# State stage of a hybrid decoder trunk: one run of small steps and one of dense blocks in each gap of the chunk chain

## The chip, the cores and the metric

The kernel runs on one core of one Trainium2 chip. The metric is the device time of one execution in microseconds; times of a kernel are the median of several runs. The profile is one execution taken by the hardware profiler.

## The reference, cut to what matters

Two layers of a decoder trunk are computed for a prompt of 1024 positions and a sample group of 8 sequences with 4 positions each. Each layer has one combined projection, a recurrent branch (RWKV-7), an attention branch with a window of 128, a merge of both, and a feed-forward part with a short convolution. The part that matters here is the recurrence of the first branch, for 8 heads of size 64:

```python
def step(S, inp):
    r_t, w_t, k_t, v_t, kk_t, a_t = inp
    sk = jnp.einsum('bhvk,bhk->bhv', S, kk_t)
    S = (S * w_t[:, :, None, :]
         - sk[..., None] * (kk_t * a_t)[:, :, None, :]
         + v_t[..., None] * k_t[:, :, None, :])
    return S, jnp.einsum('bhvk,bhk->bhv', S, r_t)
```

All data is float32. The output has the trunk's result, the new states and the new caches.

## The kernel before, in words

The recurrence is computed in chunks of 64 positions. Inside a chunk it becomes matrix products with masked Gram matrices and the inverse of a triangular matrix; between chunks the state S is carried on. A layer has 16 chunks; two of them, 128 positions, are a group `sg` (0 to 7). In this document the chunks of a layer are numbered 0 to 15: group `sg` has the chunks 2`sg` and 2`sg`+1.

`m_chain` (line 682) is the chain of a group. For each chunk TensorE first multiplies values and old state into two PSUM tiles (lines 704 and 711), VectorE copies the sum to X (line 716), TensorE multiplies it with the inverse (line 720), ScalarE writes the result as U (line 723), TensorE forms the new state (line 726), which VectorE adds up (line 730), and the output (line 733), which ScalarE copies to Y (line 737). Between these steps TensorE would wait for the other engines. So `m_chain` calls `gap(i)` at three places of each chunk: 0 after X, 1 after U, 2 after Y. What `gap` puts there decides the order of TensorE's work, since the stage runs under a manual schedule for TensorE: its instructions stay in the order in which the program writes them. For the other engines the scheduler sets the order, by its own timeline.

Three generators and one block provide the work for the gaps:

- `fill()` issues one **dense block**: three matmuls of 128x128 by 352 columns (lines 383 to 385) of the combined projection, for parts that are used only after this stage. Eight blocks fill a PSUM tile, which VectorE scales to `gt` (line 390); their total number is fixed, and what is left over runs in the attention stage.
- `nxt` is `prep(sg + 1)`, the work ahead of the next group's chain. `m_front` (line 566) loads BK, RA and VV, forms four groups of Gram products (line 590), masks them on VectorE (line 600), scales BK on GpSimd (line 604), transposes BK (line 609) and VV (line 617), and ScalarE empties these tiles (lines 612, 614, 620). `m_comb` (line 655) combines the parts of the inverse in six steps (lines 668, 673, 678). A `yield` ends a step; `yield True` says that a block should follow before the next one.
- `smp` is `m_sample` (line 852), the same work for the sample group (lines 820 to 904). `post` is `m_post` (line 908), the normalisation of a finished group on VectorE and ScalarE and its transposes (line 933).
- `inv` is `m_invs` (line 627), the inverse for the group after next: 31 columns, each with a product and a subtraction on VectorE (lines 641 and 643), then two trips through DRAM. It yields after every `IV` = 7 columns.

`psG`, `psT`, `psV`, `psY`, `psS`, `psT1` are PSUM tiles of one pool with three banks; a fourth tile has to wait until the first of them has been emptied. The chain's own tiles `xb` and `sb` have a bank each, the dense blocks two.

`gap(i)` before (lines 770 to 776) issues `HK[i]` blocks, 6, 5 and 5, and behind each of the first three a small step, `side()`. That is 16 blocks and up to nine small steps a chunk. `side()` (lines 760 to 768) takes the steps from `nxt` first and later in a chunk pair mostly from `post` and `smp`. Behind the blocks of gaps 0 and 1 one call of `inv` emits seven columns.

Of the kernel before, what the change touches and what calls it, by code (L numbers as in the profile page):

```python
# [25 lines left out]
AD = (1, 4, 4)  # L26
SQ = ((1, 3, 5, 7),) * 3
MS = 20
HK = (6, 5, 5)
AK = (4, 2)  # L30
GPB = 2
OXB = 3
# [2 lines left out]
A0 = 24  # L35
PA = (2, 2, 3, 1)
M7 = 12
GN = (3, 3, 3)
GS = 3
IV = 7  # L40
PS = 5
L = 2
TP = 1024
NS = 8
# [89 lines left out]
class Trunk:  # L134
# [492 lines left out]
    def m_invs(self, l, sg):  # L627
# [9 lines left out]
        for j in range(31):  # L637
# [5 lines left out]
            V.tensor_tensor(R[:, 0:c, j + 1:32], R[:, 0:c, j + 1:32], tv, ALU.subtract)  # L643
            if j % IV == IV - 1:
                yield
# [98 lines left out]
    def m_stage(self, l, Ts):  # L744
        ms = [{} for _ in range(8)]

        def prep(sg):
            yield from self.m_front(l, sg, ms[sg])
            yield from self.m_comb(l, sg, ms[sg], Ts[sg])
        self.fill(MS)  # L750
        for _ in prep(0):
            self.fill(1)
        self.m_state()
        smp, post = self.m_sample(l), iter(())
        for sg in range(8):
            nxt = prep(sg + 1) if sg < 7 else iter(())
            n = [0]
            cur = [None]

            def side():  # L760
                n[0] += 1
                o = (nxt,) if not sg else (nxt, smp, post) if n[0] < PS else (smp, post, nxt) if n[0] % GS == 0 else (post, nxt, smp)
                for g in (cur[0],) if cur[0] else o:
                    r = next(g, 0)
                    if r == 0 and r is not False:
                        continue
                    cur[0] = g if r else None
                    return

            def gap(i):  # L770
                for k in range(HK[i]):
                    self.fill()
                    if k < GN[i]:
                        side()
                if i < 2:
                    next(inv, 0)
            inv = self.m_invs(l, sg + 2) if sg < 6 else iter(())
            next(nxt, 0)
            Y = self.m_chain(l, sg, ms[sg], gap)
            while cur[0]:  # L780
                self.fill()
                side()
            for _ in post:
                self.fill()
            for _ in nxt:
                self.fill()
            if sg < 6:
                Ts.append(list(inv)[-1])
            if sg == 0:
                for _ in range(5):  # L790
                    next(smp)
                    self.fill()
            post = self.m_post(l, sg, Y)
            next(post)
        for _ in smp:
            self.fill()
        self.fill(M7)
        for _ in post:
            self.fill()
# [846 lines left out]
```

## Time and profile before

| | |
|---|---|
| median of 3 runs | 3429.51 us (3418.05 to 3434.38) |
| profiled execution | 3434.58 us, span 3432.8 us |
| mean granted clock of TensorE | 0.972 of full speed |
| TensorE busy | 3270.1 us (95%) |
| VectorE busy | 2220.3 us (65%) |
| ScalarE busy | 1447.6 us (42%) |
| GpSimd busy | 1361.2 us (40%) |

The state stage runs twice, once in each layer. Counted from the start of the span, the chain of layer 0 starts at 324.7 us and its chunk 15 at 640.4 us; in layer 1 these are 2021.1 and 2333.0 us. The views below name engines PE (TensorE's matmuls), PEld (its weight loads), DVE (VectorE), ACT (ScalarE) and POOL (GpSimd). A clock of 1.00 is 2.4 GHz, one of 0.50 is 1.2 GHz; values between them are means over a stretch.

### The profile page before, as it was taken

How to read it: one execution, taken by the hardware profiler on the slowest of the kernel's cores; microseconds unless marked ns; L12 is line 12 of the kernel's file. 1: busy time of each engine (PE TensorE's matmuls, PEld its weight loads, DVE VectorE, ACT ScalarE, POOL GpSimd, SP SyncE). 2: the span in 40 equal slices, each digit the busy share in tenths (PEclk: the TensorE clock that was granted, in tenths of full speed). 3: DMA queues.
4: the chain of work that ended last, by engine and by line, in shares of the span. 5: the costliest groups of instructions: out<-in, count | busy, mean ns of one | idle time of the engine just before them, and what ended most of it. 6: DMA issues, size and time to landing. Idle time of an engine off the chain costs nothing. (4 is left out here: it accounts for less than half of the span.)

```text
span 3432.8 us, 67390 instructions
## 1 busy us (share of the span) xinstructions
PE 3270.1 (95%) x26254; PEld 3064.3 (89%) x26254; DVE 2220.3 (65%) x4183; ACT 1447.6 (42%) x2908; POOL 1361.2 (40%) x1440
## 2 busy tenths in 40 slices
PE   7999889999989999999999998899999899998998
PEld 7998668888989999999999986689889899998998
DVE  6677775375567777755547778735745677777554
ACT  4443223355444444445434432243643444444443
POOL 5541121132346666633245411111323466665332
PEclk9999889999999999999999998999999999999999
DMA  3335333444542222366623453335454422225664
GB/s 116 118 117 168 104 111 113 146 152 160 179 162 75 75 77 85 103 211 214 183 92 106 136 150 107 112 108 182 138 191 143 142 75 76 86 82 174 197 187 129
DMA packets 299711, 453.48 MB, mean 132 GB/s; under 512 B 86192, under 2 KB 215728, under 8 KB 299104
## 3 DMA queue, kind: packets, MB, share of 16 engines
q1 hardware_dynamic: 298240, 448.92, 41.2%
q8 instruction: 206, 3.38, 0.4%
q14 instruction: 113, 0.93, 0.1%
q10 hardware_dynamic: 1152, 0.26, 0.0%
HBM read 322.58 MB, written 128.53 MB: 131 GB/s over the span
## 5 line engine op out<-in xcount | busy, mean ns | idle before, releaser
L1262 PE MATMUL psA<-x,wh 128*128 128x264 f32 x1408 | 404.2, 287 | 31.0 <-ACT wh L1213 21.4
L231 PE MATMUL psd<-hi,wh 128*128 128x352 f32 x1248 | 407.4, 330 | 5.1 <-ACT hi L252 2.7
L233 PE MATMUL psd<-hi,wl 128*128 128x352 f32 x1248 | 407.2, 326 | 2.7 <-POOL wl L224 1.5
L232 PE MATMUL psd<-lo,wh 128*128 128x352 f32 x1248 | 406.9, 326 | 2.0 <-DVE lo L253 2.0
L1264 PE MATMUL psA<-x,wl 128*128 128x264 f32 x1408 | 403.2, 287 | 1.4 <-DVE wl L1214 1.4
L1263 PE MATMUL psA<-x,wh 128*128 128x264 f32 x1408 | 402.9, 286 | 0.0
L383 PE MATMUL psg<-hi,wh 128*128 128x352 f32 x1056 | 388.3, 368 | 7.9 <-DVE gt L390 7.9
L1213 ACT CAST wh<-wr 128x512 fp32r<-128x512 f32 (+1 forms) x420 | 246.3, 592 | 297.6 <-PE psd L1391 178.8
L384 PE MATMUL psg<-lo,wh 128*128 128x352 f32 x1056 | 350.5, 332 | 0.0
L385 PE MATMUL psg<-hi,wl 128*128 128x352 f32 x1056 | 348.9, 330 | 0.0
L1390 PE MATMUL psd<-ap,wh 128*128 128x352 f32 x1056 | 343.0, 325 | 5.5 <-ACT wh L1213 5.4
L1391 PE MATMUL psd<-ap,wh 128*128 128x352 f32 x1056 | 342.8, 325 | 1.8 <-DVE ap L1246 1.8
L1392 PE MATMUL psd<-ap,wl 128*128 128x352 f32 x1056 | 341.9, 324 | 0.1
L1214 POOL TENSOR_TENSOR wl<-wr,wh 128x512 fp32r<-128x512 f32 (+1 forms) x196 | 248.1, 1266 | 179.3 <-ACT wh L1213 174.8
L1262 PEld LDWEIGHTS psA<-x,wh 128*128 128x128 f32 x1408 | 268.1, 190 | 33.5 <-ACT wh L1213 22.0
L1214 DVE TENSOR_TENSOR wl<-wr,wh 128x512 fp32r<-128x512 f32 (+1 forms) x224 | 167.4, 752 | 189.4 <-ACT wh L1213 187.0
L1264 PEld LDWEIGHTS psA<-x,wl 128*128 128x128 f32 x1408 | 267.6, 190 | 2.2 <-DVE wl L1214 2.0
L1263 PEld LDWEIGHTS psA<-x,wh 128*128 128x128 f32 x1408 | 268.0, 190 | 0.2
L383 PEld LDWEIGHTS psg<-hi,wh 128*128 128x128 f32 x1056 | 203.3, 193 | 51.0 <-issue 28.9
L231 PEld LDWEIGHTS psd<-hi,wh 128*128 128x128 f32 x1248 | 235.9, 190 | 9.9 <-ACT wh L223 4.0
L233 PEld LDWEIGHTS psd<-hi,wl 128*128 128x128 f32 x1248 | 236.3, 189 | 5.0 <-DVE wl L224 2.3
L232 PEld LDWEIGHTS psd<-lo,wh 128*128 128x128 f32 x1248 | 236.7, 190 | 4.5 <-DVE lo L253 3.4
(356 smaller groups left out, 8567.1 us busy)
## 6 DMA issues: line engine op xcount, KB each, us to landing
wr<-wdn SPq DMA_DIRECT2D x96, 512.0 KB, 3.5
wr<-wff SPq DMA_DIRECT2D x88, 512.0 KB, 4.0
wr<-win SPq DMA_DIRECT2D x72, 512.0 KB, 3.7
ad<-ct SPq DMA_DIRECT2D x44, 528.0 KB, 2.9
ar<-ad SPq DMA_DIRECT2D x132, 176.0 KB, 3.3
td<-gt SPq DMA_DIRECT2D x96, 176.0 KB, 1.8
gl<-td SPq DMA_DIRECT2D x32, 528.0 KB, 4.6
wr<-wdn SPq DMA_DIRECT2D x40, 384.0 KB, 3.6
```

What stands on the lines that cost most here:

```text
L231: self.nc.tensor.matmul(ps, wh, xh[:, s], start=i == 0, stop=False)
L232: self.nc.tensor.matmul(ps, wh, xl[:, s], start=False, stop=False)
L233: self.nc.tensor.matmul(ps, wl, xh[:, s], start=False, stop=i == last)
L383: nc.tensor.matmul(ps, wh[:, k], hi[:, s], start=k == 0, stop=False)
L384: nc.tensor.matmul(ps, wh[:, k], lo[:, s], start=False, stop=False)
L385: nc.tensor.matmul(ps, wl[:, k], hi[:, s], start=False, stop=k == 7)
L1214: sub.tensor_tensor(lo, x, h.bitcast(F32), ALU.subtract)
L1262: nc.tensor.matmul(ps[c][:, 0:HC], w[0][:, ws], xh, start=first and i == 0, stop=False, skip_group_check=True)
L1263: nc.tensor.matmul(ps[c][:, 0:HC], w[0][:, ws], xl, start=False, stop=False, skip_group_check=True)
L1264: self.lastP = nc.tensor.matmul(ps[c][:, 0:HC], w[1][:, ws], xh, start=False, stop=end and i == 3, skip_group_check=True)
L1390: nc.tensor.matmul(ps, wh[:, ws], hi, start=k == 0, stop=False)
L1391: nc.tensor.matmul(ps, wh[:, ws], lo, start=False, stop=False)
```

## The change

`GP` is a table with one string for each gap of a chunk pair: `n` is a step of `nxt`, `m` a step of `smp`, `p` a step of `post`, `f` a dense block. In each string all small steps come first and the blocks behind them. A step of `nxt` is no longer followed by a block of its own; `step()` still puts a block behind each `yield True` of `smp` and `post`. A pair has 6 + 5 + 4 and 5 + 5 + 6 = 31 blocks, and all 13 remaining steps of `nxt`: the seven of `m_front` in the even chunk, the six of `m_comb` in the odd one. `m_invs` yields after each column, and each of the first 30 blocks of a pair is followed by one column's emission. `HK`, `GN`, `GS`, `PS`, `side()` and the loop behind the chain go.

```diff
--- before.py
+++ after.py
@@ -26,7 +26,7 @@
 AD = (1, 4, 4)
 SQ = ((1, 3, 5, 7),) * 3
 MS = 20
-HK = (6, 5, 5)
+GP = ('nnmffffff', 'nnmfffff', 'nnnpmffff', 'nnfffff', 'nnfffff', 'nnffffff')
 AK = (4, 2)
 GPB = 2
 OXB = 3
@@ -35,10 +35,7 @@
 A0 = 24
 PA = (2, 2, 3, 1)
 M7 = 12
-GN = (3, 3, 3)
-GS = 3
-IV = 7
-PS = 5
+IV = 1
 L = 2
 TP = 1024
 NS = 8
@@ -754,32 +751,28 @@
         smp, post = self.m_sample(l), iter(())
         for sg in range(8):
             nxt = prep(sg + 1) if sg < 7 else iter(())
-            n = [0]
-            cur = [None]
-
-            def side():
-                n[0] += 1
-                o = (nxt,) if not sg else (nxt, smp, post) if n[0] < PS else (smp, post, nxt) if n[0] % GS == 0 else (post, nxt, smp)
-                for g in (cur[0],) if cur[0] else o:
-                    r = next(g, 0)
-                    if r == 0 and r is not False:
-                        continue
-                    cur[0] = g if r else None
-                    return
+            ni = [0]
+
+            def step(g):
+                while next(g, None):
+                    self.fill()
 
             def gap(i):
-                for k in range(HK[i]):
-                    self.fill()
-                    if k < GN[i]:
-                        side()
-                if i < 2:
-                    next(inv, 0)
+                for k in GP[3 * c[0] + i]:
+                    if k == "f":
+                        self.fill()
+                        ni[0] += 1
+                        if ni[0] <= 30:
+                            next(inv, 0)
+                    elif k == "n":
+                        next(nxt, 0)
+                    elif sg:
+                        step(post if k == "p" else smp)
+                c[0] += i == 2
+            c = [0]
             inv = self.m_invs(l, sg + 2) if sg < 6 else iter(())
             next(nxt, 0)
             Y = self.m_chain(l, sg, ms[sg], gap)
-            while cur[0]:
-                self.fill()
-                side()
             for _ in post:
                 self.fill()
             for _ in nxt:
```

Three places show how instructions move. Line numbers of the changed kernel are smaller by 3, behind `m_stage` by 7. The first is TensorE in chunk 11 of layer 0, where `m_comb` works: `psT` are its PSUM tiles, `TB` and `Tt` its operands, `psg` the dense blocks. Before:

```order
L668 MATMUL psT_7226<-con,Tt_397 32x32 x8
L383 MATMUL psg<-hi,wh 128x352
L384 MATMUL psg<-lo,wh 128x352
L385 MATMUL psg<-hi,wl 128x352
L673 MATMUL psT_7175<-TB,GB 32x32 x8
L383 MATMUL psg<-hi,wh 128x352
L384 MATMUL psg<-lo,wh 128x352
L385 MATMUL psg<-hi,wl 128x352
L673 MATMUL psT_7226<-TB,GB 32x32 x8
```

Now, behind the last matmul of line 711 (708 in the changed kernel):

```order
L708 MATMUL xb_7169<-st_4131,RA 64x64
L665 MATMUL psT_7199<-con,Tt_397 32x32 x8
L665 MATMUL psT_7210<-con,Tt_397 32x32 x8
L380 MATMUL psg<-hi,wh 128x352
L381 MATMUL psg<-lo,wh 128x352
L382 MATMUL psg<-hi,wl 128x352
```

Both halves of the first step now follow one another, and five blocks follow them. The steps of lines 673 and 678 stand in pairs in the other two gaps of the chunk.

The second place is TensorE in the last gap of chunk 10, from the last matmul of the chain's output (line 733, now 730). Before:

```order
L733 MATMUL xb_7435<-UV,GB 64x64
L383 MATMUL psg<-hi,wh 128x352
L384 MATMUL psg<-lo,wh 128x352
L385 MATMUL psg<-hi,wl 128x352
L609 MATMUL psT<-con,BK 128x128 x4
L383 MATMUL psg<-hi,wh 128x352
L384 MATMUL psg<-lo,wh 128x352
L385 MATMUL psg<-hi,wl 128x352
L617 MATMUL psV<-con,VV 128x128 x4
```

Now:

```order
L730 MATMUL xb_6913<-UV,GB 64x64
L606 MATMUL psT<-con,BK 128x128 x8
L614 MATMUL psV<-con,VV 128x128 x4
L926 MATMUL psY<-con,Y 128x128 x4
L380 MATMUL psg<-hi,wh 128x352
L381 MATMUL psg<-lo,wh 128x352
L382 MATMUL psg<-hi,wl 128x352
```

Eight transposes of BK, four of VV and the four of the finished output `Y` (which stood in the gap ahead of it) follow the chain's output without a block between; they write four tiles of the pool with three banks. Four blocks follow.

The third is VectorE in chunk 2 of layer 0, where the sample group's state is read (`big` and `Xs`, lines 873 and 874, now 866 and 867). `GB` is the mask multiply of line 600, `it` and `R` are the inverse. Before:

```order
L847 TENSOR_TENSOR Rs<-Rs,its 8x8x3
L600 TENSOR_TENSOR GB<-psG_4744,con 128x4x128
L600 TENSOR_TENSOR GB<-psG_4745,con 128x4x2x64
L641 TENSOR_TENSOR it<-R,Lt 128x31
L643 TENSOR_TENSOR R<-R,it 128x31
L641 TENSOR_TENSOR it<-R,Lt 128x30
```

The inverse goes on there for 24 rows, up to the next pair of `GB`. Now:

```order
L840 TENSOR_TENSOR Rs<-Rs,its 8x8x3
L597 TENSOR_TENSOR GB<-psG_4735,con 128x4x128
L597 TENSOR_TENSOR GB<-psG_4736,con 128x4x2x64
L866 TENSOR_TENSOR big<-psS_4753,con 64x512
L867 TENSOR_REDUCE Xs<-big 64x64
L866 TENSOR_TENSOR big<-psS_4754,con 64x512
L638 TENSOR_TENSOR it<-R,Lt 128x31
L867 TENSOR_REDUCE Xs<-big 64x64
```

Two multiplies and two reductions of the sample group stand right behind the pair of `GB`; 22 rows of the inverse, with one `gt` among them, stand between it and the next pair.

Counted over chunks 0 to 14 of a layer, TensorE has 249 dense blocks before and 243 now; groups of tiled matmuls (32 or 64 rows or columns of the array) that stand together without a block or a full transpose between are 131 before and 57 now.

## Rows read from the trace of the kernel before

**Rows 1.** The page, part 1: busy time and share of the span by engine.

```profile
PE 3270.1 (95%) x26254; PEld 3064.3 (89%) x26254; DVE 2220.3 (65%) x4183; ACT 1447.6 (42%) x2908; POOL 1361.2 (40%) x1440
```

**Rows 2.** Stretches of the stages: length, busy us (instructions), clock, DMA share, GB/s.

```profile
324.70:545.40 220.70, 193.64 (x2144) 151.13 (x2143) 169.32 (x529) 61.77 (x149) 39.31 (x43) 0.90 0.36 101
545.40:640.40 95.00, 94.41 (x1261) 80.07 (x1260) 33.48 (x65) 35.07 (x87) 15.56 (x16) 1.00 0.34 101
2021.10:2238.10 217.00, 192.03 (x2144) 150.37 (x2143) 168.47 (x532) 61.71 (x149) 38.60 (x43) 0.89 0.37 104
2238.10:2333.00 94.90, 94.31 (x1261) 80.02 (x1260) 32.26 (x61) 35.05 (x87) 15.55 (x16) 1.00 0.32 100
```

**Rows 3.** Timeline of TensorE, chunk 9: start us, us, instruction.

```profile
549.42 0.43 PE L383 MATMUL psg<-hi,wh 128*128 128x352 f32 x1
...
550.10 0.69 PE L673 MATMUL psT<-TB,GB 32*32 32x32 f32 x16
...
557.21 0.69 PE L726 MATMUL sb<-UV,Bt 128*64 128x64 f32 x16
557.83 0.68 PE L733 MATMUL xb<-UV,GB 64*64 64x64 f32 x16
558.44 0.43 PE L383 MATMUL psg<-hi,wh 128*128 128x352 f32 x1
...
559.03 0.33 PE L383 MATMUL psg<-hi,wh 128*128 128x352 f32 x1
...
559.51 0.32 PE L383 MATMUL psg<-hi,wh 128*128 128x352 f32 x1
```

**Rows 4.** The same timeline, chunk 10.

```profile
562.10 0.69 PE L711 MATMUL xb<-st,RA 64*64 64x64 f32 x32
562.72 0.43 PE L383 MATMUL psg<-hi,wh 128*128 128x352 f32 x1
...
568.37 0.68 PE L720 MATMUL xb<-X,Tt 64*64 64x64 f32 x16
568.99 0.43 PE L383 MATMUL psg<-hi,wh 128*128 128x352 f32 x1
...
575.09 0.60 PE L609 MATMUL psT<-con,BK 128*128 128x128 f32 x4
575.45 0.41 PE L383 MATMUL psg<-hi,wh 128*128 128x352 f32 x1
```

**Rows 5.** Groups by line on VectorE, chunks 0 to 8 of layer 0.

```profile
L643 DVE TENSOR_TENSOR R<-R,it 128x66 f32<-128x66 f32 (+24 forms) x192 | 53.2, 277 | 5.2
L641 DVE TENSOR_TENSOR it<-R,Lt 128x66 f32<-128x66 f32 (+24 forms) x193 | 47.4, 245 | 14.2 <-POOL R L636 4.7 <-DMA Lt<-ld 4.6
```

**Rows 6.** Waits of TensorE's loads, layers 0 and 1: us, times, longest us.

```profile
PEld psG L590 <- DVE GB L600: 14.6, 5, 6.0
...
PEld psG L590 <- DVE GB L600: 20.3, 5, 6.0
```

**Rows 7.** Waits of VectorE, chunks 0 to 8 of layer 0.

```profile
DVE st L730 <- PE sb L726: 8.2, 3, 6.8
DVE gt L390 <- PE psg L385: 7.5, 6, 2.9
DVE it L641 <- POOL R L636: 4.7, 2, 4.0
...
DVE big L873 <- PE psS L870: 3.8, 3, 3.1
```

**Rows 8.** Timeline of ScalarE, end of chunk 10.

```profile
574.60 0.76 ACT L737 COPY Y<-xb 64x256 f32<-64x256 f32 x2 [0.53 <-PE xb L733]
575.73 0.37 ACT L612 COPY Bt<-psT 128x256 f32<-128x256 f32 x1 [0.36 <-PE psT L609]
576.11 0.75 ACT L614 COPY Bt<-psT 64x256 f32<-64x256 f32 x2
```

**Rows 9.** Stretch of chunk 2, layer 0 (columns of rows 2).

```profile
364.30:397.30 33.00, 23.39 (x239) 17.58 (x238) 25.58 (x71) 7.43 (x17) 5.63 (x6) 0.84 0.41 111
```

## The prediction

> **What bounds the kernel now.** I read the busy shares first: TensorE is busy for 95% of the span [rows 1], so time can only go where TensorE waits, runs at its lower clock, or does work that another order makes cheaper. Next comes the table by stretches, for the two state stages. I number the chunks of a layer 0 to 15 (two for each group of 128 positions). Chunks 0 to 8, which carry the sample group and six of the eight inverses, take 220.7 and 217.0 us in the two layers, with TensorE busy for 193.6 and 192.0 us and a granted clock of 0.90 and 0.89; chunks 9 to 14 take 95.0 and 94.9 us, TensorE is busy throughout and the clock is 1.00 [rows 2]. So there are two kinds of stretch, and the change has to be costed in each by itself.
>
> In chunks 9 to 14 the order of TensorE's own work is the price. The timeline there shows it. Dense blocks that follow one another start 0.48 us apart (559.03 to 559.51). A block that stands alone between two groups of small matmuls takes 0.68 us from its start to the start of the next group (549.42 to 550.10) [rows 3]. So each change to small tiles and back costs 0.20 us on the dense side. On the small side a group of 32 small matmuls takes 0.62 us to the next block (562.10 to 562.72) and one of 16 takes 0.62 us too (568.37 to 568.99) [rows 4]: much of a group is its start and its end. But two groups of different shape behind one another keep the full price: 0.62 us from L726 to L733, then 0.61 us [rows 3].
>
> In chunks 0 to 8 VectorE is the partner. It is busy for 169.3 of 220.7 us [rows 2], and the two lines of the inverse alone are 100.6 us of that [rows 5]. The table of waits shows both engines waiting for each other: TensorE waits for the mask multiply of line 600 for 14.6 us in layer 0 and 20.3 us in layer 1, five times each and up to 6.0 us [rows 6]. VectorE in turn waits for TensorE, in its three largest rows 8.2, 7.5 and 3.8 us, 19.5 us together, and 4.7 us for GpSimd's copy [rows 7].
>
> **The change, part by part.** *Grouping.* By the order of instructions, a layer has 131 groups of tiled matmuls (everything that is not a dense block or a full 128x128 transpose) in chunks 0 to 14 before, and 57 after: 88 become 39 in chunks 0 to 8, and 43 become 18 in chunks 9 to 14. What each merged group saves is at least the 0.20 us of the dense side. The small side adds between nothing (different shapes, 0.62 and 0.61 us) and, for equal shapes, some 0.15 us: a bound from the 16 and the 32 matmuls that both take 0.62 us, taken well short of it because the moving operand of line 590 is twice as wide. I take 0.25 us, nearer to the row of the lone block, and keep 0.20 and 0.35 us as ends.
>
> *Blocks.* A pair of chunks issues 31 dense blocks in its gaps instead of 32, and a few of the extra blocks behind long steps go too. Chunks 0 to 8 issue 150 blocks instead of 153, chunks 9 to 14 issue 93 instead of 96. That is 1.4 us less in each stretch (3 x 0.48) and 2.9 us more in the attention stage, since the number of blocks is fixed. I cost them there in full. (If they fill holes there, they are free: 0 is the other end.)
>
> *New waits in a group.* In the third gap of an even chunk four PSUM tiles are now written behind one another: two of transposes, the values, and the finished output. The pool has three banks, so the fourth waits until ScalarE has emptied the first. ScalarE first copies Y (0.76 us), then empties a transpose tile (0.37 + 0.75 us), 1.9 us in all; TensorE meanwhile has three groups of 0.36 us to do, 1.1 us [rows 4, 8]. So 0.8 us, with the semaphore on top 1.0 us, for each even chunk with such a step; in chunks 9 to 14 these are chunks 10 and 12, 2.0 us. The ends are 0, if ScalarE's copies come earlier, and 3.5 us each, the mean of the ten waits of rows 6.
>
> *Chunks 9 to 14* then give 25 x 0.25 + 1.4 - 2.0 = 5.7 us a layer.
>
> *Chunks 0 to 8.* TensorE needs 49 x 0.25 + 1.4 = 13.7 us less. Whether the stretch gets shorter hangs on VectorE, whose work is the same. It can shrink only by the time in which VectorE waits for TensorE, of which 19.5 us are shown [rows 7]; its wait for GpSimd stays. I take 12 us: most of what TensorE saves, short of the rest, because part of the merged groups stands where TensorE has to wait anyway. Ends: 0 and 19.5 us.
>
> *The inverse by columns* I cost at nothing. VectorE's order is set by the scheduler, not by where a column is emitted, and there single columns stand between the other instructions already; in chunk 2 a run of 24 rows of the inverse stands ahead of the second pair of mask multiplies before, and one of 22 after. If the finer emission did shorten a wait of TensorE behind such a run, it would be one of rows 6; that is in the case of the larger gain. *SP's queue.* The loads and stores keep their number and change places. The one that can be late is the load of the next group's RA and BK, issued ahead of the chain as before: line 590 now follows the state matmuls with no block between, so it comes up to 0.68 us earlier [rows 3], 4.8 us a layer over seven even chunks if every load landed that late. I take 0, since the waits of line 590 that the view of rows 6 lists as large are for VectorE, not for a load.
>
> **The sum.** 12 + 5.7 - 2.9 = 14.8 us a layer, 29.6 us for both. The profiled execution took 3434.58 us (span 3432.8), which gives 3405.0. It stands 5.1 us above the median of the three runs, 3429.51; I take half of that off: **3402 us**. Its own range, with 0.20 or 0.35 us a group and 7 to 15 us in chunks 0 to 8, is 3384 to 3418. What a measurement can tell here is about 0.5%, 17 us: 3412.4 is the bound to faster and 3446.7 the one to slower.
>
> **Rivals.** *VectorE sets the pace* (no gain in chunks 0 to 8). For it: VectorE is busy for 77% of that stretch [rows 2], in an order with fixed places, and the change moves its work into the even chunks, where its order has the mask multiplies, the sample group and 22 rows of the inverse behind one another. Against it: 19.5 us of waits for TensorE. Then the gain is 2 x (5.7 - 2.9) = 5.6 us: 3429.0, less the half offset 3426. No change that can be measured.
>
> *VectorE's waits go altogether* (19.5 us, and the extra blocks fill holes in attention): 2 x (19.5 + 5.7) = 50.4 us, 3384.2, with the offset 3382. For it: the second mask multiply now has six dense blocks and the transition matmuls to hide behind, where one block stood between the two groups of line 590 in which the waits of rows 6 end.
>
> *Slower: grouped steps wait for banks and TensorE's clock falls.* The place is the sample step that now stands right behind the groups of line 590 with no block between (gaps 0 and 1 of chunks 2, 6 and 8). Both write the same three banks, so the step waits for the mask multiply, and all dense blocks stand behind it. A wait costs 3.5 us (34.9 us over ten) [rows 6]. The clock costs more: in chunk 2, with such waits in it, it was 0.84 over 33.0 us, against 1.00 in chunks 9 to 14 [rows 2, 9]; 0.90 over 220.7 us and 0.89 over 217.0 us are together 46 us of full-speed time, at most 4.6 us for each of the ten waits. So a new wait costs up to 8.1 us, and from two of them in a layer on the 14.8 us are gone. Three in each layer: 3434.6 - 29.6 + 6 x 8.1 = 3453.6, with the offset 3451. Against it: the waits that are there now end at the same multiplies, so some are replaced and not added; and where VectorE is the slower engine, a lower clock hides behind it. The Trainium skill, "TensorE: Matmul & The Clock Gate", section "A second HAM failure mode: psum-queue depth-cycling", describes this: a kernel that cycles through PSUM banks pauses TensorE between groups of matmuls so often that its clock goes up and down between the two levels. By that rule the grouping is worse than the interleaving; the trace agrees so far as the clock falls in stretches with waits and nowhere in chunks 9 to 14.
>
> That the change does not do what it says I can leave out for the groups, since the order shows them; for the inverse it is what I assume.
>
> **How the numbers follow.** The forecast 0.52 (0.46 of it under 3412, 0.06 above), waits gone altogether 0.14, VectorE sets the pace 0.23, slower 0.11. Faster by over 0.5%: 0.46 + 0.14 = 0.60; within: 0.06 + 0.23 = 0.29; slower: 0.11. The range 3376 to 3438 takes in the forecast, most of the larger gain and the case without gain; it leaves out the slower case and the end of the larger gain.
>
> **What would show it.** In the changed profile: lone blocks of 0.68 us gone from chunks 9 to 14, which should take 88 to 90 us at clock 1.00, with a wait of about 1 us ahead of the last transposes of chunks 10 and 12; chunks 0 to 8 between 203 and 210 us, VectorE's rows of waits for TensorE about half, its busy time unchanged; attention some 3 us longer. It would be wrong if chunks 0 to 8 stayed at 217 to 221 us (VectorE), or if the clock of chunks 9 to 14 fell below 1.00, or chunks 2 to 8 had more and longer waits for line 600 than ten.

## The result, and the profile after

| | before | changed kernel |
|---|---|---|
| median, same comparison | 3423.78 us (3417.65 to 3434.38, 4 runs) | 3382.91 us (3381.54 to 3387.12, 4 runs) |
| profiled execution | 3434.58 us, span 3432.8 us | 3382.31 us, span 3380.4 us |
| mean granted clock | 0.972 | 0.976 |

The ratio is 0.9879, with an interval from 0.9849 to 0.991: the change makes the kernel 40.9 us, or 1.2%, faster. The two profiled executions are 52.4 us apart in span, because the one of before stands at the long end of its runs. What follows splits these 52.4 us.

The first view is the page's busy time by engine, of the changed kernel.

```profile
PE 3217.4 (95%) x26254; PEld 3054.1 (90%) x26254; DVE 2222.4 (66%) x4183; ACT 1445.1 (43%) x2908; POOL 1354.8 (40%) x1440
```

Beside [rows 1] this holds the whole result: TensorE issues the same 26254 matmuls and is busy for 52.7 us less (3270.1 to 3217.4). Its idle time, the span less this, is 162.7 us before and 163.0 us now. In the sums, the time came out of TensorE's busy time and not out of its waits; the experiments show that two opposite effects stand behind this.

The next view is the table by stretches of the changed kernel: chunks 0 to 8 and 9 to 14 of layer 0, then of layer 1 (columns as in [rows 2]).

```profile
326.50:521.20 194.70, 170.13 (x2127) 142.39 (x2126) 166.97 (x522) 61.35 (x151) 36.16 (x42) 0.95 0.42 115
521.20:608.50 87.30, 85.09 (x1260) 77.61 (x1259) 36.18 (x69) 34.15 (x84) 16.29 (x16) 1.00 0.36 106
1986.10:2189.10 203.00, 174.94 (x2128) 146.46 (x2128) 161.53 (x507) 59.75 (x146) 35.20 (x41) 0.90 0.40 110
2189.10:2279.70 90.60, 87.80 (x1262) 80.09 (x1261) 39.04 (x84) 35.54 (x89) 16.58 (x17) 0.96 0.37 104
```

Against [rows 2], chunks 0 to 8 are 26.0 us shorter in layer 0 and 14.0 us in layer 1, chunks 9 to 14 7.7 and 4.3 us. The rest of a layer hardly moved: the first chain starts 1.8 us later (324.7 to 326.5), from chunk 15 of layer 0 to the chain of layer 1 it takes 1377.6 us instead of 1380.7, and from there to the end 1100.7 instead of 1099.8. The sum is -52.0 +1.8 -3.1 +0.9 = -52.4.

In chunks 0 to 8 TensorE's busy time fell by 23.5 and 17.1 us. Its idle time (length less busy) went from 27.1 to 24.6 us in layer 0 and from 25.0 to 28.1 us in layer 1: 52.0 us for both before, 52.6 now. That sum alone would read as if no wait had been touched. The table of TensorE's waits in the changed kernel, chunks 0 to 8, layer 0 above and layer 1 below, tells otherwise.

```profile
PE psS L863 <- DVE GB L597: 5.2, 2, 3.3
PE xb L717 <- DVE X L713: 3.2, 6, 1.0
PE ubs L876 <- DVE Xs L873: 2.7, 1, 2.7
...
PE psS L863 <- DVE GB L597: 9.1, 2, 5.9
PE ubs L876 <- DVE Xs L873: 5.1, 1, 5.1
PE xb L717 <- DVE X L713: 4.4, 5, 2.4
...
PE psG L587 <- DVE GB L597: 0.2, 1, 0.2
```

The Gram products' wait for the mask multiply, the largest row before [rows 6], has gone but for 0.2 us (1.2 us by the waits of the loads, which [rows 6] lists). The sample step (line 863, tile `psS`) now waits longer for the same multiply, now line 597: 14.3 us over both layers, 16.5 us by its loads. It stands right behind the Gram products and needs the next bank of the same pool. This wait is not new in layer 0. Before, the sample step's loads (then line 870) already waited for the multiply for 6.7 us, nearly all of it there; layer 0 above, layer 1 below:

```profile
PEld psS L870 <- DVE GB L600: 6.5, 2, 6.1
...
PEld psS L870 <- DVE GB L600: 0.2, 1, 0.2
```

VectorE's largest waits in the same stretch of layer 0 are:

```profile
DVE it L638 <- POOL R L633: 5.5, 5, 1.6
DVE big L866 <- PE psS L863: 4.6, 3, 2.9
DVE its L838 <- DMA Rs<-idr: 3.2, 1, 3.2
DVE st L727 <- PE sb L723: 1.5, 2, 1.1
```

All its waits for TensorE come to 23.8 us in layer 0 before and 7.4 us now, in layer 1 to 22.5 and 9.6 us. [Rows 7] has the largest of before.

In chunk 10 of layer 0 the order can be read from TensorE's timeline (start us, us, instruction, idle before it and releaser).

```profile
538.72 1.06 PE L587 MATMUL psG<-RA,BK 64*64 64x128 f32 x32
539.70 0.43 PE L380 MATMUL psg<-hi,wh 128*128 128x352 f32 x1
...
542.22 0.32 PE L380 MATMUL psg<-hi,wh 128*128 128x352 f32 x1
...
542.54 0.32 PE L382 MATMUL psg<-hi,wl 128*128 128x352 f32 x1
542.79 0.62 PE L717 MATMUL xb<-X,Tt 64*64 64x64 f32 x14
...
548.10 1.09 PE L606 MATMUL psT<-con,BK 128*128 128x128 f32 x8
549.03 0.60 PE L614 MATMUL psV<-con,VV 128*128 128x128 f32 x4
550.14 0.66 PE L926 MATMUL psY<-con,Y 128*128 128x128 f32 x4 [0.51 <-ACT Bt L611]
```

Six blocks stand together there. From the start of the first to the small group behind the last it is 3.09 us (539.70 to 542.79), 0.21 us more than six times the 0.48 us of a block in a run: the price of an edge is paid once for the six, not once for each lone block as in [rows 3]. Two groups of Gram products behind one another take 0.98 us to the next block (538.72 to 539.70). One group alone took 0.59 us in chunk 10 before:

```profile
563.41 0.67 PE L590 MATMUL psG<-RA,BK 64*64 64x128 f32 x16
564.00 0.43 PE L383 MATMUL psg<-hi,wh 128*128 128x352 f32 x1
```

The wait ahead of the last transposes is there, with 0.51 us. ScalarE's copies at that place run from 548.20 to 550.09 us; the first and the last of them are:

```profile
548.20 0.75 ACT L734 COPY Y<-xb 64x256 f32<-64x256 f32 x2 [1.77 <-PE xb L730]
...
549.34 0.75 ACT L611 COPY Bt<-psT 64x256 f32<-64x256 f32 x2
```

### The profile page after: what moved, and what is told of

It is laid out like the page before. It is cut to its first block, busy times and chain, and to the rows that moved or that the text cites. A ratio compares the mean times of both kernels' runs of the same rounds, so it can differ in the third digit from the quotient of the medians.

```text
span 3380.4 us, 67406 instructions
## 1 busy us (share of the span) xinstructions
PE 3217.4 (95%) x26254; PEld 3054.1 (90%) x26254; DVE 2222.4 (66%) x4183; ACT 1445.1 (43%) x2908; POOL 1354.8 (40%) x1440
## 5 line engine op out<-in xcount | busy, mean ns | idle before, releaser
L380 PE MATMUL psg<-hi,wh 128*128 128x352 f32 x1056 | 366.3, 347 | 6.4 <-DVE gt L387 6.4
```

Of the source, the lines that this page charges most:

```text
L380: nc.tensor.matmul(ps, wh[:, k], hi[:, s], start=k == 0, stop=False)
```

## The experiments

The kernels were run on three chips, each time beside runs of before, whose medians there lie between 3424.5 and 3426.9 us. Times below are medians; ratios are to before, with their intervals. For the main ones, this is what their table by stretches gives for chunks 0 to 8, both layers added (idle is length less busy). Each row is one profiled execution, which can lie some 11 us from the kernel's median: that of before lies 10.8 us above it, that of the ungrouped kernel with the late sample step 9.4 us.

| kernel | length | TensorE busy | TensorE idle |
|---|---|---|---|
| before | 437.7 | 385.7 | 52.0 |
| changed kernel | 397.7 | 345.1 | 52.6 |
| ungrouped, new places | 411.0 | 378.9 | 32.1 |
| sample step late | 371.9 | 334.1 | 37.8 |
| ungrouped, sample step late | 398.4 | 373.5 | 24.9 |
| every product in gap 0 | 425.6 | 358.2 | 67.4 |
| half of the inverse | 382.5 | 344.2 | 38.3 |

### The same steps in the same gaps, but not grouped

```diff
-GP = ('nnmffffff', 'nnmfffff', 'nnnpmffff', 'nnfffff', 'nnfffff', 'nnffffff')
+GP = ('fnfnfmfff', 'fnfnfmff', 'fnfnfnpmf', 'fnfnfff', 'fnfnfff', 'fnfnffff')
```

> The changed kernel with the same steps and the same number of dense blocks in every gap, but each small step between two blocks again: 89 and 44 groups of tiled matmuls in chunks 0 to 8 and 9 to 14 (39 and 18 in the changed kernel, 88 and 43 before); the inverse is still emitted by columns. If the grouping is the cause, chunks 9 to 14 go from 87 to 90 us back to 94 to 97 us and chunks 0 to 8 from 195 to 203 us to 213 to 221 us: about 3420 us. If another part of the change (which step stands in which gap, the emission of the inverse) made the gain of chunks 0 to 8, these stay at 195 to 205 us and only chunks 9 to 14 grow by 7 to 9 us a layer: about 3400 us.

Measured: 3402.48 us, ratio 0.9921 (0.9896 to 0.9945). Its stretches:

```profile
324.80:520.50 195.70, 185.74 (x2127) 144.82 (x2126) 156.97 (x499) 58.89 (x143) 35.14 (x41) 0.93 0.41 112
520.50:614.80 94.30, 93.20 (x1262) 78.86 (x1261) 40.28 (x92) 35.41 (x90) 17.41 (x16) 1.00 0.36 104
1999.40:2214.70 215.30, 193.14 (x2127) 149.41 (x2126) 165.07 (x529) 58.89 (x143) 35.20 (x41) 0.90 0.37 102
2214.70:2308.10 93.40, 93.03 (x1261) 78.78 (x1260) 33.17 (x60) 35.36 (x89) 17.42 (x16) 1.00 0.36 104
```

About half of the gain, 19.6 us, is the grouping; the other half is there without it. In chunks 9 to 14 of layer 0, at clock 1.00 in both, TensorE's busy time is 93.20 us here and 85.09 us in the changed kernel, 8.1 us for 26 groups (44 and 18): 0.31 us a group. In chunks 0 to 8 grouping takes 33.8 us of busy time (378.9 to 345.1) and puts 20.5 us of idle time back. So the change has two parts that the totals hide: new places for the steps take 19.9 us of TensorE's idle time away (52.0 to 32.1), and grouping, with the sample step in the group, brings as much back. The gain of the new places is uneven: chunks 0 to 8 fall from 220.7 to 195.7 us in layer 0 and only from 217.0 to 215.3 us in layer 1 [rows 2], though both layers run the same program. And since the profiled execution of before is a long one, its size is better read from the medians on this chip, 24.4 us (3426.87 to 3402.48).

### The inverse seven columns at a time again

```diff
-IV = 1
+IV = 7
...
-                        ni[0] += 1
-                        if ni[0] <= 30:
-                            next(inv, 0)
...
+                if i < 2:
+                    next(inv, 0)
```

> The changed kernel with the emission of the inverse as before: seven columns at a time, at the end of gaps 0 and 1. As I costed it, nothing changes: 3383 us, within 7 us, chunks 0 to 8 at 195 to 205 us. If the emission by columns is worth something, chunks 0 to 8 grow by 5 us a layer or more, all waits for VectorE: 3393 us or more.

Measured: 3382.25 us, ratio 0.9863 (0.9837 to 0.9889); chunks 0 to 8 take 196.9 and 200.3 us. The emission by columns is worth nothing that can be measured. The run also shows that a kernel as fast as the changed one gives the same time on the chip on which the ungrouped and the late sample step ran.

### The sample step behind the dense blocks

```diff
-GP = ('nnmffffff', 'nnmfffff', 'nnnpmffff', 'nnfffff', 'nnfffff', 'nnffffff')
+GP = ('nnffffffm', 'nnfffffm', 'nnnpffffm', 'nnfffff', 'nnfffff', 'nnffffff')
```

> The changed kernel with the sample group's step behind the dense blocks of its gap and not ahead of them, so that the mask multiply of line 597 has the blocks to run beside. If the waits for PSUM banks cost time, TensorE's waits of line 863 for that multiply (5.2 us in layer 0, 9.1 us in layer 1) go, and the time falls by 6 to 14 us: 3369 to 3377 us. If VectorE sets the pace in chunks 0 to 8, TensorE waits the same time elsewhere: 3383 us, within 5 us.

Measured: **3356.5 us** (3355.79 to 3363.6), ratio 0.9794 (0.9771 to 0.9818): 2.1% below before and 26.4 us below the changed kernel, the best of all. Chunks 0 to 8:

```profile
325.40:512.40 187.00, 169.79 (x2127) 146.01 (x2126) 153.70 (x488) 61.02 (x150) 36.58 (x41) 0.92 0.44 120
...
1978.90:2163.80 184.90, 164.28 (x2127) 140.73 (x2126) 148.90 (x471) 59.88 (x147) 35.37 (x40) 0.94 0.43 118
```

And the waits of TensorE there, layer 0 and layer 1:

```profile
PE psG L587 <- DVE big L866: 3.5, 1, 3.5
PE ubs L876 <- DVE Xs L873: 2.5, 1, 2.5
PE psS L863 <- DVE GB L597: 2.0, 1, 2.0
...
PE psG L587 <- DVE big L866: 6.5, 1, 6.5
...
PE psS L863 <- DVE GB L597: 1.0, 1, 1.0
```

The gain is about twice the 6 to 14 us that were expected. The wait of line 863 falls from 14.3 to 3.0 us, though 10.0 us of it come back as a wait of line 587 for the sample step's own multiply. In the table idle falls by 14.8 us, so most of it is in smaller waits that these rows do not show: line 863's waits for other tiles and for DMAs (5.5 us) are gone, and line 717 waits 3.8 us instead of 7.6. Busy time falls by 11.0 us, nearly all of it in layer 1 (174.94 to 164.28 us for x2128 and x2127 matmuls), where the clock went from 0.90 to 0.94; in layer 0 the clock fell from 0.95 to 0.92 and the busy time stayed. So the place of the sample step cost the change 26 us, of which some 11 are busy time of the same matmuls.

### The same late sample step, not grouped

```diff
-GP = ('nnmffffff', 'nnmfffff', 'nnnpmffff', 'nnfffff', 'nnfffff', 'nnffffff')
+GP = ('fnfnffffm', 'fnfnfffm', 'fnfnfnpfm', 'fnfnfff', 'fnfnfff', 'fnfnffff')
```

> The kernel with the late sample step (3356.5 us) with a block between any two small steps again, as in the run without grouping. If the grouping is worth about 0.25 us for each of the tile changes saved wherever they stand, chunks 9 to 14 grow by 6 to 7 us and chunks 0 to 8 by 10 to 13 us a layer: 3390 to 3397 us. If in chunks 0 to 8 VectorE's pace hides it, only chunks 9 to 14 grow: 3369 to 3372 us.

Measured: 3391.36 us, ratio 0.9906 (0.9884 to 0.9929). With the sample step late in both, grouping is worth 34.9 us (38 us by the two ratios, since they ran on different chips). In the table it takes 39.4 us of busy time and puts back 12.9 us of idle time (by a profiled execution that is 9.4 us longer than the median).

### Half of the inverse

The loop over columns takes every second one, so 15 of 31 columns are not computed.

```diff
-        for j in range(31):
+        for j in range(0, 31, 2):
...
-                        if ni[0] <= 30:
+                        if ni[0] <= 30 and ni[0] % 2 == 0:
```

> The changed kernel with every second column of the inverse left out (16 of 31), so VectorE has some 50 us less to do in chunks 0 to 8 of each layer; what is computed is not the inverse. If VectorE sets the pace there (busy for 167 of 195 us), the stretch falls to what TensorE needs by itself, about 165 to 175 us: 3383 less 50 to 65 us, about 3325 us. If TensorE sets it, only its shown waits for VectorE can go, about 10 us a layer: about 3363 us.

Measured: 3360.93 us, ratio 0.9805 (0.9779 to 0.9832). Chunks 0 to 8:

```profile
324.50:517.20 192.70, 172.51 (x2127) 145.85 (x2126) 116.27 (x306) 59.82 (x146) 35.34 (x40) 0.90 0.42 115
...
1979.90:2169.70 189.80, 171.65 (x2127) 145.19 (x2126) 114.99 (x306) 59.81 (x146) 35.41 (x40) 0.91 0.42 117
```

VectorE is busy for 50.7 and 46.5 us less, and the stretches are 2.0 and 13.2 us shorter. The time is the one of the second case, but the work did not become less everywhere. These are chunks 2 to 4 and 6 to 8 of layer 0 in the changed kernel, and then in this run:

```profile
362.20:439.50 77.30, 62.08 (x751) 52.41 (x750) 64.23 (x200) 22.45 (x53) 9.33 (x11) 0.89 0.43 117
456.60:521.20 64.60, 58.23 (x695) 45.91 (x694) 59.04 (x178) 20.49 (x53) 17.62 (x19) 0.97 0.42 119
...
358.70:440.90 82.20, 65.83 (x749) 55.52 (x748) 64.04 (x192) 22.38 (x53) 9.92 (x12) 0.81 0.43 116
460.80:517.20 56.40, 54.83 (x695) 43.74 (x694) 25.51 (x47) 18.37 (x46) 14.76 (x15) 1.00 0.42 123
```

In chunks 2 to 4, where most of TensorE's idle time stands (15.2 of 24.6 us in the changed kernel), VectorE is as busy as before, so the run says nothing on its weight there, and the wait of line 863 for the mask multiply is still there (7.7 us in layer 0). In chunks 6 to 8 VectorE is busy for 33.5 us less, and the stretch is 8.2 us shorter: it ends 1.6 us above TensorE's busy time, at clock 1.00. In layer 1 these are 29.9 and 11.3 us, with the same 1.6 us left. So VectorE's total is not what sets the pace of the nine chunks, and where its work was taken away, what came back was TensorE's waits and its clock, not the work that was saved.

### Two steps in gap 0 and four in gap 1, in the kernel before

```diff
-GN = (3, 3, 3)
+GN = (2, 4, 3)
```

> The kernel before with one edit: two small steps in gap 0 and four in gap 1 (three and three before), so that the third group of line 590, which needs the bank of the first, stands behind the blocks of gap 0 and line 720; groups of tiled matmuls and blocks keep their number. If that place is what the change gained besides the grouping, TensorE's waits of line 590 for the mask multiply (14.6 and 20.3 us) go, chunks 0 to 8 fall from 217 to 221 us to 200 to 208 us, and the time is 3390 to 3405 us; chunks 9 to 14 stay at 95 us. If the waits only move (VectorE sets the pace), the time stays at 3427 us, within 8 us.

Measured: 3429.68 us, ratio 1.0017 (1.0002 to 1.0031); chunks 0 to 8 take 219.3 and 218.6 us. The waits of TensorE's loads in layer 0 and layer 1:

```profile
PEld psS L870 <- DVE GB L600: 12.9, 2, 12.4
...
PEld psG L590 <- DVE GB L600: 2.8, 2, 2.2
...
PEld psS L870 <- DVE GB L600: 6.6, 2, 6.2
...
PEld psG L590 <- DVE GB L600: 6.2, 4, 2.8
```

The waits of [rows 6] fell from 34.9 to 9.0 us and nothing was won. The sample step waits for the same multiply for 19.5 us now (6.7 us before), and TensorE's idle time in these chunks is 50.0 us instead of 52.0 (length less busy, both layers). The expected gain failed: a bank that is emptied late is waited for by whichever step needs it next.

### Every Gram product in gap 0

```diff
-GP = ('nnmffffff', 'nnmfffff', 'nnnpmffff', 'nnfffff', 'nnfffff', 'nnffffff')
+GP = ('nnnnffffffm', 'fffffm', 'nnnpffffm', 'nnfffff', 'nnfffff', 'nnffffff')
```

> The kernel with the late sample step (3356.5 us) with all four groups of Gram products in gap 0 of the even chunk, so that the third waits at once for the mask multiply of the first. Groups and blocks keep their number. If their place matters, TensorE waits some 2 us or more in front of the blocks in each of seven even chunks of a layer: 3375 to 3395 us. If VectorE's pace hides it, the time is 3357 us, within 6 us.

Measured: 3401.32 us, ratio 0.9936 (0.9921 to 0.995), 44.8 us above the best version, from which it differs by the place of two steps. The load's wait in layer 0:

```profile
PEld psG L587 <- DVE GB L597: 21.3, 5, 6.5
```

This is the wait of [rows 6] back in the grouped order: the product groups behind the first need banks whose mask multiply VectorE still has in its queue. In the table idle goes to 67.4 us. The time lies 6 us beyond the expected range.

### The output's transposes and the sample step at other places

Two more tables were tried on the best version. The first moves the step of `post` behind two blocks of gap 2, against the wait of 0.51 us shown above.

```diff
-GP = ('nnmffffff', 'nnmfffff', 'nnnpmffff', 'nnfffff', 'nnfffff', 'nnffffff')
+GP = ('nnffffffm', 'nnfffffm', 'nnnffpffm', 'nnfffff', 'nnfffff', 'nnffffff')
```

> The kernel with the late sample step (3356.5 us) with the finished output's step (post) behind two of the four blocks of its gap, so that its PSUM tile finds a bank. The shown waits of line 926 for ScalarE (some 5 us over both layers) go: 3350 to 3354 us. If they hide behind VectorE's pace, 3356 us, within 4 us.

Measured: 3368.39 us, ratio 0.9846 (0.9828 to 0.9864), 11.9 us above the best version. Chunks 10 and 12 became shorter as meant, from 15.5 to 14.8 us, but chunk 6 takes 31.9 and 34.3 us instead of 25.6 and 25.4:

```profile
446.40:478.30 31.90, 27.37 (x243) 18.75 (x242) 26.59 (x79) 8.69 (x21) 9.25 (x9) 0.84 0.36 105
```

The expectation failed. The clock in that chunk is 0.84, where it was 1.00 in the best version, and VectorE is busy there for 26.6 us instead of 22.1; chunk 4 became shorter, from 26.0 and 27.6 to 23.1 and 23.0 us. Why the loss is in chunk 6 is not settled.

The second moves the sample step of gap 0 to the end of the pair:

```diff
-GP = ('nnmffffff', 'nnmfffff', 'nnnpmffff', 'nnfffff', 'nnfffff', 'nnffffff')
+GP = ('nnffffff', 'nnfffffm', 'nnnpffffm', 'nnfffff', 'nnfffff', 'nnffffffm')
```

> The changed kernel with the sample group's steps late in gaps 1 and 2 of the even chunk and at the end of the odd one (the late form had all three in the even chunk, 3356.5 us). VectorE is busy for 28 of 36 us in chunk 2 and for 12 of 15 us in chunk 3 of the changed kernel. If chunks 2 to 8 are held up by that uneven load, they get 2 to 3 us shorter a pair: 3342 to 3352 us. If the waits of single steps count and not the load, 3357 us, within 7 us.

Measured: 3387.05 us, ratio 0.9883 (0.9863 to 0.9903); chunks 0 to 8 take 196.9 and 207.8 us. This failed too, by 30.6 us against the best version.

### The sample step kept to the even chunk, in the kernel before

The order by `n[0]` is changed so that behind the ninth step of a pair no sample step is taken, as in the changed kernel.

```diff
-GN = (3, 3, 3)
+GN = (2, 4, 3)
...
-                o = (nxt,) if not sg else (nxt, smp, post) if n[0] < PS else (smp, post, nxt) if n[0] % GS == 0 else (post, nxt, smp)
+                o = (nxt,) if not sg else (nxt, smp, post) if n[0] < PS else (nxt, post) if n[0] > 9 else (smp, post, nxt) if n[0] % GS == 0 else (post, nxt, smp)
```

> The kernel before with two steps in gap 0 and four in gap 1 (3429.7 us) and, besides, no sample step taken in an odd chunk while a step of the next group is left, which is nearly the distribution of the changed kernel without its grouping (that took 3402.5 us). If this distribution is what the change gained besides the grouping, chunks 0 to 8 fall to 200 to 210 us: 3400 to 3412 us. If not, 3428 us, within 8 us.

Measured: 3419.31 us, ratio 0.9975 (0.996 to 0.9989). Chunks 0 to 8 take 211.6 and 196.3 us, 29.8 us less than before, but chunks 9 to 14 take 101.6 and 103.0 us, 14.7 us more: sample steps that no longer fit move there, and with 2106 and 2108 matmuls instead of 2144 the first stretch also has less to do. The time lies between the two cases. It shows the direction of the part that is not grouping, not its size.

### No sample step in the chain, grouped and not

In both, the sample group's steps run behind the chain. The changed kernel's table loses its `m`; in the kernel before, `side()` no longer takes `smp`.

```diff
-GP = ('nnmffffff', 'nnmfffff', 'nnnpmffff', 'nnfffff', 'nnfffff', 'nnffffff')
+GP = ('nnffffff', 'nnfffff', 'nnnpffff', 'nnfffff', 'nnfffff', 'nnffffff')
```

```diff
-                o = (nxt,) if not sg else (nxt, smp, post) if n[0] < PS else (smp, post, nxt) if n[0] % GS == 0 else (post, nxt, smp)
+                o = (nxt,) if not sg else (nxt, post) if n[0] < PS or n[0] % GS == 0 else (post, nxt)
```

> The changed kernel with all sample steps behind the chain of the last group, each with a block behind it. Chunks 2 to 8 then have no sample work on TensorE and VectorE and no PSUM tiles of it. If the sample's waits for banks hold these chunks up, they fall to 14 to 17 us each, 135 to 150 us for chunks 0 to 8, and the end of the stage grows by 25 to 35 us: about 3350 us, within 15 us. If VectorE's inverse sets the pace, chunks 0 to 8 stay above 165 us: 3385 us or more.

> The kernel before with all sample steps behind the chain of the last group. Beside the run with the same edit on the changed kernel it shows what the grouping alone is worth: 119 groups of tiled matmuls in chunks 0 to 14 against some 46, and 6 blocks more. At 0.25 to 0.35 us a group and 0.48 us a block (given back later), the two differ by 37 to 51 us. Chunks 2 to 8 at 15.6 and 17.6 us as chunks 9 to 13 if nothing else holds them up.

Measured: 3421.32 us, ratio 0.998 (0.9964 to 0.9995), grouped, and 3460.39 us, ratio 1.0092 (1.0074 to 1.011), not grouped. The first lies far above the expected 3350 us, and its chunks 0 to 8 take 161.7 and 163.4 us, more than the 135 to 150 expected. Both end later than their originals, since the sample steps now run behind the chain: from chunk 15 of layer 0 to the chain of layer 1 it takes 1428.2 us instead of 1377.6 grouped, and 1421.5 instead of 1380.7 not grouped. The difference of the two times is 39.1 us. It is not the grouping alone, since the two also differ in the places of the steps of `nxt` and in the emission of the inverse. Chunks 0 to 8 of layer 0, grouped:

```profile
324.20:485.90 161.70, 148.82 (x2019) 132.55 (x2018) 129.85 (x432) 57.05 (x139) 27.84 (x30) 0.95 0.42 118
```

and not grouped:

```profile
326.40:511.30 184.90, 165.37 (x2042) 137.01 (x2041) 136.41 (x451) 58.80 (x144) 31.43 (x33) 0.94 0.39 106
```

At nearly the same clock, TensorE is busy for 16.6 us less and idle for 6.6 us less. With the sample step out of the way, the changed kernel has no added idle time to pay for its grouping. The grouped profile is of the shortest execution, 11.2 us below the median.

## Why the prediction was right, and where not

The sign, the bound of 0.5% and the range held: 3382.9 us lies between 3376 and 3438. The forecast of 3402 was 19 us too slow, and its own range (3384 to 3418) just misses the result. That range does not follow from the ends that it names: 0.20 or 0.35 us a group and 7 to 15 us give 3391 to 3415, with the offset. The gain was 40.9 us where 29.6 was forecast, and only about half of it has the forecast cause, the grouping: that the range held is in part luck.

**Grouping saves TensorE's work: right.** Three pairs that differ in grouping differ by 19.6, 34.9 and 39.1 us, in the order in which bank waits are taken out of the grouped side. Only the first two differ in nothing else.

**The price of a group: mis-sized.** "I take 0.25 us, nearer to the row of the lone block" should have been 0.31, within the ends of 0.20 and 0.35. What was taken too low is the small side. Two groups of line 587 now take 0.98 us where one alone in a gap took about 0.6, so groups of the same shape share their ends. For the 74 merged groups of a layer that is 4.4 us, 8.9 for both layers. This is the price in busy time. In the whole time the merged groups gave less in the changed kernel, 19.6 us against the ungrouped one with 76 more groups in each layer, or 0.13 us each, because of the waits that came with them.

**Chunks 9 to 14: right in layer 0, and in part in layer 1.** 5.7 us forecast, 7.7 and 4.3 measured, at 87.3 and 90.6 us where 88 to 90 was promised. The wait for the fourth PSUM tile is there with 0.5 us, not 1.0, in chunk 10. ScalarE's copies took 1.9 us, as worked out, but TensorE's twelve transposes ahead of it took 1.5 us to their end and not 1.1; and the 0.2 us for the semaphore, for which the prediction had no row, are not there: the transposes start 0.05 us behind the copy (550.09 to 550.14). Layer 1 falls short, and its clock is 0.96 there and not 1.00 as promised, which the prediction had named as a sign of being wrong, because chunk 9 takes 19.4 us instead of 15.6: VectorE is busy for 161.5 us in chunks 0 to 8 of layer 1 instead of 168.5, and for 39.0 instead of 32.3 behind them, so it enters chunk 9 with work left over.

**Chunks 0 to 8: the step that failed.** The text said: "It can shrink only by the time in which VectorE waits for TensorE, of which 19.5 us are shown", and took 12 us. The stretches gave 26.0 and 14.0. The cap was too low and built on waits that move. Layer 0 went past it: VectorE's waits for TensorE fell by 16.4 us there (the three rows of the cap left out 4.3 of 23.8 us), and those for GpSimd and DMAs, which I held fixed, by 6.4 (15.4 to 9.0). In layer 1 the former fell by 12.9 us and the latter rose by 8.3 (12.5 to 20.8). What can be worked out ahead is TensorE's busy time, which fell by 23.5 and 17.1 us: 49 groups at 0.31 and 1.4 us for three blocks are 16.6 us, and layer 1, where the clock stayed (0.89 and 0.90), has 17.1 us. Layer 0 has 6.4 us more, where the clock rose from 0.90 to 0.95: 2144 matmuls before and 2127 now, at a higher clock. TensorE's idle time hardly moved, but only since two effects cancel that the prediction did not have as such, 19.9 us less by the new places and 20.5 us more by the grouping.

**Attention: the other end.** 2.9 us a layer were forecast for the extra blocks, with 0 as the other end. The parts behind the chains changed by -3.1 and +0.9 us: 0 holds.

**The inverse by columns: right.** It is worth nothing, as emission by sevens shows.

**The rivals.** "VectorE sets the pace" is refuted by the result: chunks 0 to 8 are 26.0 and 14.0 us shorter while VectorE's busy time there fell by 2.4 and 6.9 us. That its queue holds TensorE up in single chunks is not refuted; the half inverse shows it for chunks 6 to 8. "VectorE's waits go altogether" gave 3382 us and met the time, and partly the mechanism: the waits fell by two thirds and by more than half, attention cost nothing, but they did not go, and more came from the work itself. The slower rival has its mechanism in the trace: the sample step behind the Gram products waits for their bank, up to 3.3 us in layer 0 and 5.9 us in layer 1. The clock in chunk 2 is 0.86 over 35.7 us, longer than before [rows 9], and in layer 1 it is 0.78 over 39.1 us, where chunk 2 took 25.9 us at 0.87 before:

```profile
362.20:397.90 35.70, 24.28 (x248) 18.53 (x247) 28.36 (x79) 8.89 (x21) 4.23 (x5) 0.86 0.45 132
397.90:412.70 14.80, 14.59 (x225) 13.34 (x224) 12.27 (x42) 4.99 (x12) 2.04 (x3) 1.00 0.64 148
...
2021.20:2060.30 39.10, 24.71 (x246) 18.69 (x245) 28.52 (x77) 8.89 (x21) 4.57 (x6) 0.78 0.40 110
```

Chunk 3 of layer 0, the second row, then takes 14.8 us at 1.00, where it took 26.6. So the even chunk pays and the odd one is shorter, but in part because work has moved: chunk 3 has 225 of TensorE's instructions now and had 291. This mechanism cost 26.4 us, shown by the sample step moved late; the rival had priced it at 6 x 8.1 = 48.6 us. What I wrote against it, that some waits are replaced and not added, holds for the line in question: the waits of [rows 6] went, 33.7 of their 34.9 us, and those of the sample step's loads grew by 9.8. The rule of the Trainium skill that stood beside that rival ("TensorE: Matmul & The Clock Gate", "A second HAM failure mode: psum-queue depth-cycling") is borne out by the lower clock where these waits are, but not as a verdict against grouping: grouped is faster than not grouped in all three pairs.

**What I did not see.** About half of the gain is no grouping at all. It comes from which step stands in which gap: TensorE's idle time falls from 52.0 to 32.1 us with the new places alone, nearly all of it in layer 0 (27.1 to 10.0). I had costed the new places only where they add a wait. Which of the moves it is stays open. Two steps instead of three in gap 0 do not do it in the kernel before; keeping the sample step to the even chunk gives some of it and gives half back later.

## What to carry to other kernels

Where small tiled matmuls fill the gaps of a dense stream, put those of one gap behind one another and the dense blocks behind them: each merged group took 0.31 us off TensorE's busy time here, and how much of that reached the kernel's time hung on the waits that came with it. Then look at every step at the end of such a run, and if the bank it needs is emptied by work that an engine still has in its queue, put it behind the dense blocks: here that one move was worth 26.4 us on top. When two engines wait for each other, cost a change by the busy and the idle time of the engine that carries the path, chunk by chunk: taking away half of VectorE's inverse (97 us over both layers) made these chunks 15 us shorter, and the gain stood in chunks 6 to 8, where it took TensorE's waits away.

## What was not expected of the hardware

- Groups of small matmuls of the same shape share their ends: 0.98 us for two groups of line 587 in chunk 10, and 32 matmuls of line 670 take 1.03 us to the next block (558.02 to 559.05) where 16 took 0.62.
- Full 128x128 transposes have no such price, and so nothing to save. Four and the lone block behind them took 0.92 us, from the start of line 609 at 575.09 [rows 4] to the row at the end of this section. Eight together take 0.93 us to the next tile (548.10 to 549.03), so four of them 0.46, and with the 0.48 us of a block in a run that is 0.94 us.
- Less waiting gave TensorE's matmuls more than the wait in one case and not in another. With the sample step late, idle time in chunks 0 to 8 fell by 14.8 us and the busy time of the same matmuls by 11.0 us, nearly all in the layer whose clock rose (0.90 to 0.94). With half of the inverse, idle time fell by 14.3 us and the busy time by 0.9 us, at a clock of 0.90 and 0.91 instead of 0.95 and 0.90.

The start of the next transposes in chunk 10 of before:

```profile
576.01 0.60 PE L617 MATMUL psV<-con,VV 128*128 128x128 f32 x4
```
